# Ordering every engine's work by the scheduler's timeline model in a two-layer RWKV-7 / Conformer backbone

## The chip, the cores and the metric

The kernel runs on one core of a Trainium2 chip. The metric is the device time of one execution in microseconds (us); less is better. A core has a matrix engine (PE), a vector engine (DVE), an activation engine (ACT), GpSimd (POOL) and SyncE (SP), each with an instruction stream of its own that it works off strictly in order. The engines meet only at semaphores. SP and POOL mostly issue DMAs. So for a program whose instructions are given, the order of the instructions on each engine is what is left to choose.

## What is computed

The model has two layers over 512 latent tokens and a prefix of 256 context tokens, D = 1024, all in fp32 at the interface. Layer 0 is the even mixer; it has sixteen heads of 64, which the kernel takes as eight pairs, and a recurrence with a 64x64 state per head, in both directions:

```python
def wkv_scan(S0, r, decay, k, v, kk, a, reverse):
    def step(S, inp):
        r_t, w_t, k_t, v_t, kk_t, a_t = inp
        sa = jnp.einsum("bhvk,bhk->bhv", S, -kk_t)
        S = (S * w_t[:, :, None, :]
             + sa[..., None] * (kk_t * a_t)[:, :, None, :]
             + v_t[..., None] * k_t[:, :, None, :])
        return S, jnp.einsum("bhvk,bhk->bhv", S, r_t)
...
    r, k, v, za, bg, cg, xb, zb = jnp.split(h @ w_in, EVEN_SPLITS, axis=-1)
    ya, _, _ = rwkv_seq(rwkv_prep(h, r, k, v, *rw), S_f, S_b, r_k, lnx_w, lnx_b, True)
    yb = bg * dwconv(cg * xb, sc_w, seg_len)
    y = jnp.concatenate([ya.astype(h.dtype) * jax.nn.silu(za), yb * jax.nn.silu(zb)], axis=-1) @ w_out
```

The context tokens are run first and give the start states S_f and S_b. Layer 1 is a Conformer module (two gated projections, a 31-tap depthwise convolution, a layer norm, an output projection) on the latent tokens alone.

## The kernel before

**Projections.** Each of the eight column groups of h @ w_in (r, k, v, za, bg, cg, xb, zb) is cut into eight blocks of 128 columns. One block is 24 matmuls of 128x512 on PE (`proj`, L361): eight k-tiles, and three products for each, because operands are split into a high and a low fp32r part (`hilo`, L117: a DMA at L123, a cast on ACT at L126, a subtraction on DVE at L127). In the trace the accumulators are called pcg, pxb, pbg and pzb, the operands hlh, hll, whxb, wlxb and so on.

**The recurrence.** It is worked in chunks of 64 tokens. Four context stages of four steps come first (two head pairs each, `chain_ctx`, L689), then eight latent stages of eight steps (one head pair each, `chain_lat`, L739). One latent step is a chain through three engines, and the next step needs its end:

```python
cmm(zo..., AR[z]..., H...)   # then cmm(zo..., E..., UV...)
S.copy(Zs, zo[:, 0:2, :])    # ACT, L758, Ol<-zol in the trace
cmm(uh..., E..., Zs...)
S.copy(UV..., uh...)         # ACT, L764
cmm(uh..., BKt..., UV...)
V.scalar_tensor_tensor(out=Hn..., in0=uh..., scalar=PC..., in1=HP...)   # DVE, L771
```

All matmuls of these chains are pinned to one written order over all stages (`cmm`); so are the masks' products pa (L589 to L601) and the transposes pb (L605 to L612) of each stage.

**What runs beside a chain.** While stage s walks its eight steps, the program has a triangular solve for stage s+1 (`solve`, L642: a transpose at L650, which needs four copies Nt that ACT makes at L618 from all eight E tiles of DVE's L601, then 31 pairs of a product at L656 and a sum at L658 on DVE, each needing the one before), the merge of the solved blocks (L662 to L683), the operands of stage s+2 (`light`, `heavy`, L434 to L636: decay scan L521, products L531 to L556, masks L601, transposes), the finish of stage s (group norm, L795 to L815), and the four projections of one block of the convolution branch (`conv_branch`, L825: cg, xb, bg, zb; L837 takes pxb, L841 twice does the taps, L847 takes pbg, L792 makes the gate from pzb, L850 ends it).

**What sets the order.** The kernel is written against a tile framework. It records the instructions with their data dependences; a list scheduler then picks, for each engine, the next ready instruction by a model of how long each takes, and the program's place among the instructions breaks ties. What holds in any order: the data dependences, the buffers' reuse, the pinned chains, and the few `tc.issue_after` anchors, which forbid an instruction to be placed before an instruction of the chain (CONV_AFTER = (0, 2, 7, 6): cg not before step 0, xb not before step 2, bg not before step 7, zb not before step 6; LIGHT_AFTER and HEAVY_AFTER do the same for the operands of stage s+2). The anchors set a lower bound and no upper one.

**The end.** The output projection of layer 0 has two passes over 16 k-tiles with 12 matmuls each (L130); the first pass needs no result of the last stage but for its last k-tile and lies beside it. Layer 1 follows (L975 to L1245).

## Time and profile before

| | |
|---|---|
| median of three runs | 1452.06 us (1447.48 to 1453.27) |
| the profiled execution | 1451.59 us, of which span 1449.6 us |
| mean granted PE clock | 0.979 |
| setup, first projections (0 to 224.6 us) | 224.6 us |
| four context stages (224.6 to 525.2 us) | 300.6 us |
| seven latent stages (525.2 to 928.3 us) | 403.1 us |
| last latent stage (928.3 to 957.3 us) | 29.0 us |
| rest of the output projection (957.3 to 1040.2 us) | 82.9 us |
| layer 1 (1040.2 us on) | 409.4 us |

The limits are the starts of the first matmul of each stage's chain, read from the trace; that of the output projection's end is the first matmul of layer 1. In a row of the trace, `L771` is the line, `Hl<-uh,PCl,HPl` the tile written and those read (numbers left out), then the shape, the count, the busy time and the mean in ns, and behind the last bar the idle time of the engine just before these instructions with what ended it. A PE row's duration is longer than the time that it takes from PE, since matmuls are pipelined; the distance between two starts is that time.

### The profile page before, as it was taken

Reading aid. Unit: us, or ns where it says so; the run is one execution under the profiler, and the core shown is the slowest. Engines: PE = TensorE matmul, PEld = TensorE weight load, DVE = VectorE, ACT = ScalarE, POOL = GpSimd, SP = SyncE. Lnnn points to the kernel's source line nnn. Section 1 sums busy time; section 2 is a strip of 40 time slices with the busy share of each in tenths; the row PEclk is TensorE's granted clock in tenths of the full one; section 3 lists DMA queues with packets and bytes.
Section 4 is the critical chain, followed back from the end, with each engine's and each line's share of the span. In section 5 each row is a group of like instructions: output and inputs, shape, how many; then the busy total and the mean of one; then the engine's idle time right before and its main releaser. Section 6 shows DMA issues by size and latency. Waiting matters only on the chain. (4 is left out here: it accounts for less than half of the span.)

```text
span 1449.6 us, 29729 instructions
## 1 busy us (share of the span) xinstructions
PE 1407.2 (97%) x11921; PEld 1012.7 (70%) x11921; DVE 983.7 (68%) x2294; ACT 749.5 (52%) x1516; POOL 118.2 (8%) x246
## 2 busy tenths in 40 slices
PE   6999999999998999999999999999999999999998
PEld 1564677878776766666676666778777777788876
DVE  2675597568688989999999998557745544544333
ACT  4536364364664665756666565456753323464222
POOL 2023210000101101011011100010000000000000
PEclk9999999979897999999999999999999999999999
DMA  9755433312222321222222212359803303133322
GB/s 324 221 172 160 153 110 98 97 52 71 83 85 74 92 69 59 81 86 60 76 67 83 91 49 84 131 175 324 252 34 102 117 22 95 58 102 91 99 89 86
DMA packets 137626, 158.54 MB, mean 109 GB/s; under 512 B 15375, under 2 KB 104143, under 8 KB 137369
## 3 DMA queue, kind: packets, MB, share of 16 engines
q1 hardware_dynamic: 121104, 106.47, 23.6%
q0 software_dynamic: 15312, 48.99, 10.5%
q8 instruction: 94, 1.54, 0.4%
q10 hardware_dynamic: 1072, 1.19, 0.2%
q14 instruction: 44, 0.36, 0.1%
HBM read 138.33 MB, written 18.28 MB: 108 GB/s over the span
## 5 line engine op out<-in xcount | busy, mean ns | idle before, releaser
L57 PE MATMUL o<-wh,y 128*128 128x512 f32 x248 | 79.7, 397 | 0.0
L658 DVE TENSOR_TENSOR Yl<-Yl,xtmpl 128x126 f32<-128x126 f32 (+22 forms) x248 | 62.2, 251 | 2.7
L656 DVE TENSOR_TENSOR xtmpl<-Xl,Yl 128x126 f32<-128x126 f32 (+22 forms) x248 | 62.0, 250 | 2.7
L57 PE MATMUL pal<-ARl,BKl 64*128 64x128 f32 x512 | 57.8, 306 | 5.5 <-DVE xtmpc L656 2.8
L57 PEld LDWEIGHTS pal<-ARl,BKl 64*128 64x128 f32 x512 | 42.9, 195 | 24.9 <-issue 6.0
L1140 ACT CAST ah<-a 64x512 fp32r<-64x512 f32 x32 | 19.8, 619 | 75.6 <-DVE a L1135 75.2
L57 PE MATMUL zol<-UV,E 64*64 64x64 f32 (+1 forms) x1024 | 54.0, 221 | 0.2 <-ACT UV L764 0.2
L57 PEld LDWEIGHTS o<-wh,y 128*128 128x128 f32 x248 | 45.9, 188 | 9.5
L764 ACT COPY UV<-uh 64x128 f32<-64x128 f32 x128 | 33.3, 260 | 33.5 <-PE uh L57 25.9
L57 PE MATMUL o<-wl,y 128*128 128x512 f32 x124 | 49.4, 398 | 1.2 <-DVE wl L127 1.2
L57 PE MATMUL zol<-Hl,ARl 64*64 64x64 f32 x896 | 50.2, 230 | 0.3
L57 PEld LDWEIGHTS zol<-Hl,ARl 64*64 64x64 f32 x896 | 35.0, 133 | 20.3 <-issue 16.7
L127 DVE TENSOR_TENSOR wl<-wr,wh 128x1024 fp32r<-128x1024 f32 x28 | 34.2, 1223 | 19.6 <-ACT wh L126 19.1
L1135 DVE TENSOR_TENSOR a<-pu,a 128x512 f32<-128x512 f32 x16 | 11.0, 690 | 53.0 <-PE pu L57 50.7
L57 PEld LDWEIGHTS uh<-UV,BKt 128*64 128x64 f32 x704 | 26.7, 138 | 28.5 <-ACT UV L764 23.1
L601 DVE TENSOR_TENSOR E<-pal,maskE 128x512 f32<-128x512 f32 x64 | 43.0, 685 | 3.4 <-PE pal L57 3.0
L57 PEld LDWEIGHTS zol<-UV,E 64*64 64x64 f32 (+1 forms) x1024 | 42.3, 136 | 2.5 <-ACT UV L764 2.0
L1095 DVE SCALAR_TENSOR_TENSOR pr<-px,dbe,What 119x512 f32<-119x512 f32 x32 | 22.6, 745 | 31.1 <-PE px L57 31.1
L126 ACT CAST wh<-wr 128x1024 fp32r<-128x1024 f32 x28 | 29.6, 1056 | 20.7 <-PE o L57 10.4
L771 DVE SCALAR_TENSOR_TENSOR Hl<-uh,PCl,HPl 128x64 f32<-128x64 f32 x112 | 26.4, 277 | 20.1 <-PE uh L57 9.6
L875 POOL DMA_DIRECT2D mwr<-in_mod_w_dram x56 | 29.9, 538 | 114.2 <-PE uh L57 67.4
L57 PE MATMUL uh<-UV,BKt 128*64 128x64 f32 x704 | 36.7, 234 | 2.2 <-ACT UV L764 2.2
(947 smaller groups left out, 4250.9 us busy)
## 6 DMA issues: line engine op xcount, KB each, us to landing
mwr<-in_mod_w_dram POOLq DMA_DIRECT2D x56, 256.0 KB, 3.6
wr<-in_ev_w_out_dram SPq DMA_DIRECT2D x28, 512.0 KB, 5.6
ectx<-in_mod_w_dram SPq DMA_DIRECT2D x12, 512.0 KB, 5.2
wrk<-in_ev_w_in_dram SPq DMA_DIRECT2D x16, 256.0 KB, 3.1
wrv<-in_ev_w_in_dram SPq DMA_DIRECT2D x16, 256.0 KB, 4.6
wrr<-in_ev_w_in_dram SPq DMA_DIRECT2D x16, 256.0 KB, 2.9
wrza<-in_ev_w_in_dram SPq DMA_DIRECT2D x16, 256.0 KB, 2.8
wrcg<-in_ev_w_in_dram SPq DMA_DIRECT2D x16, 256.0 KB, 2.8
```

The costliest lines, as they stand in the source:

```text
L57: return T.matmul(o, lhsT, rhs, start=start, stop=stop)
L126: S.copy(hi, raw)
L127: env["lo"].tensor_tensor(out=lo, in0=raw, in1=hi, op=ALU.subtract)
L601: V.tensor_tensor(out=E[:, h, z * NLAT + c0 : z * NLAT + c0 + m, :], in0=pas[h], in1=maskE[:, z * (1 + h) : z * (1 + h) + 1, 0:x].to_broad ...
L656: V.tensor_tensor(out=tv, in0=X[:, :i, i : i + 1].to_broadcast([P, i, m]), in1=Y[:, i : i + 1, c0:].to_broadcast([P, i, m]), op=ALU.mult)
L658: V.tensor_tensor(out=Y[:, :i, c0:], in0=Y[:, :i, c0:], in1=tv, op=ALU.add)
L764: u_ = S.copy(UV[ZR[1 - h], i : 2 * nch - i : 2 * nch - 1 - 2 * i, ZR[h]], uh[ZR[1 - h], 0:2, :])
L771: h_ = V.scalar_tensor_tensor(out=Hn[:, z, :], in0=uh[:, 2 + z, :], scalar=PC[z][:, i : i + 1], in1=HP[:, z, :], op0=ALU.mult, op1=ALU.add)
L875: nc.gpsimd.dma_start(mws[q], I["mod_w"][layer, kt * P : (kt + 1) * P, c0 : c0 + 512])
L1095: V.scalar_tensor_tensor(out=pr[s][:NPROD], in0=px[s][:NPROD], scalar=dbe[:, 0:1], in1=What[:, n * 512 : n * 512 + 512], op0=ALU.add, op1= ...
L1135: V.tensor_tensor(out=a, in0=pp[1], in1=a, op=ALU.mult)
L1140: S.copy(ahl[s][hr], a[hr])
```

## The change

One argument, in the function that builds the program:

```diff
@@ -1319,7 +1319,7 @@
     out = nc.dram_tensor("out_0_dram", (1, SEQ, D), F32, kind="ExternalOutput").ap()
-    with _tile.TileContext(nc) as tc:
+    with _tile.TileContext(nc, schedule_with_timeline_sim=True) as tc:
         tile_backbone_kernel(tc, aps, out)
```

The list scheduler stays; the model behind it is another one, with a timeline of its own for each engine. Every instruction of the kernel is there as before: PE's 8217 matmuls, DVE's and ACT's instructions, the DMAs. The pinned chains and the anchors hold as before. What differs is the order of each engine's stream, and with it some semaphore instructions. On PE the runs of fp32r matmuls (the projections) between fp32 ones (the chains and the stages' operands) are 394 before and 210 now.

The first place is PE in latent stage 3, step 2. zol3_2 is the chain's first product in this step, uh0<-Ol3 its second, uh0<-UV110 with BKt its third; pcg4 and pxb4 are projections of the convolution branch. Before:

```order
L57 MATMUL zol3_2_7905<-UV110_5057,E110_5058 64x64 x4
L57 MATMUL pcg4_8511<-hll_119,whcg40_8500 128x512
L57 MATMUL pcg4_8511<-hlh_118,wlcg40_8501 128x512
L57 MATMUL pcg4_8511<-hlh_118,whcg40_8500 128x512
L57 MATMUL pcg4_8511<-hll_119,whcg40_8500 128x512
L57 MATMUL uh0_123<-Ol3_7834,E110_5058 64x64 x4
L57 MATMUL zol3_2_7905<-Hl3_1_7894,ARl30_6576 64x64 x2
L57 MATMUL zol3_2_7905<-Hl3_1_7894,ARl31_6606 64x64 x2
L57 MATMUL pcg4_8511<-hlh_118,wlcg40_8501 128x512
L57 MATMUL pcg4_8511<-hlh_118,whcg41_8506 128x512
L57 MATMUL uh0_123<-UV110_5057,BKt111_5060 64x64 x2
```

The same place now, with twenty of the 24 rows of pxb4 left out at the mark:

```order
L57 MATMUL zol3_2_7905<-UV110_5057,E110_5058 64x64 x4
L57 MATMUL pxb4_8550<-hlh_118,whxb40_8539 128x512
L57 MATMUL pxb4_8550<-hll_119,whxb40_8539 128x512
...
L57 MATMUL pxb4_8550<-hll_119,whxb41_8545 128x512
L57 MATMUL pxb4_8550<-hlh_118,wlxb41_8546 128x512
L57 MATMUL uh0_123<-Ol3_7834,E110_5058 64x64 x4
L57 MATMUL zol3_2_7905<-Hl3_1_7894,ARl30_6576 64x64 x2
L57 MATMUL zol3_2_7905<-Hl3_1_7894,ARl31_6606 64x64 x2
L57 MATMUL uh0_123<-UV110_5057,BKt111_5060 64x64 x2
L57 MATMUL uh0_123<-UV110_5057,BKt110_5059 64x64 x2
L57 MATMUL zol3_2_7905<-UV110_5057,E110_5058 64x64 x4
```

Before, the projections stand in pieces of two to four between the chain's products of every step; now the block of 24 stands whole inside one step, and steps 3 and 4 have none. Over the eight steps of this stage PE has 24, 4, 24, 0, 4, 0, 24 and 24 fp32r matmuls, where it had 5, 6, 9, 9, 9, 2, 6 and 58.

The second place is DVE behind the last update of the state in the same stage, Hl3_6. Yl4, xtmpl4 and Xl4 belong to the solve for stage 4, ARl51 and BKl51 are operands of stage 5. Before:

```order
L771 SCALAR_TENSOR_TENSOR Hl3_6_8069<-uh0_123,PCl31_6598,HPl3_6_8037 128x64
L784 TENSOR_TENSOR Ol3_7834<-zol3_6_8045,Ol3_7834 128x2x64
L656 TENSOR_TENSOR xtmpl4_8107<-Xl4_8105,Yl4_8106 128x78
L554 TENSOR_TENSOR ARl51_8264<-rl5_8177,Pl51_8251 128x8x64
L658 TENSOR_TENSOR Yl4_8106<-Yl4_8106,xtmpl4_8107 128x6x13
L555 SCALAR_TENSOR_TENSOR BKl51_8265<-al51_8249,iPl51_8253 128x8x64
L656 TENSOR_TENSOR xtmpl4_8107<-Xl4_8105,Yl4_8106 128x70
L556 TENSOR_TENSOR BKl51_8265<-kdl51_8258,iPl51_8253 128x8x64
L784 TENSOR_TENSOR Ol3_7834<-zol3_7_8077,Ol3_7834 128x2x64
L658 TENSOR_TENSOR Yl4_8106<-Yl4_8106,xtmpl4_8107 128x5x14
```

The same place now; pzb4 and pbg4 are the projections that PE has in the steps 6 and 7:

```order
L771 SCALAR_TENSOR_TENSOR Hl3_6_8069<-uh0_123,PCl31_6598,HPl3_6_8037 128x64
L784 TENSOR_TENSOR Ol3_7834<-zol3_6_8045,Ol3_7834 128x2x64
L683 COPY E100_4354<-uh1_124 32x16x32
L127 TENSOR_TENSOR wlcg50_9330<-wrcg50_9328,whcg50_9329 128x512
L792 SCALAR_TENSOR_TENSOR gzb4_8655<-gzb4_8655,pzb4_8630 128x512
L127 TENSOR_TENSOR wlcg51_9336<-wrcg51_9334,whcg51_9335 128x512
L847 TENSOR_TENSOR yb4_8576<-pbg4_8592,yb4_8576 128x512
L601 TENSOR_TENSOR E110_5058<-pal5010_8348,maskE_108 128x512
L601 TENSOR_TENSOR E110_5058<-pal5011_8349,maskE_108 128x512
L784 TENSOR_TENSOR Ol3_7834<-zol3_7_8077,Ol3_7834 128x2x64
```

The solve of stage 4 is over before Hl3_4 now, and its merge ends with L683 right behind Hl3_6. The masks L601 of stage 5, which were the second and fourth row behind Ol3<-zol3_7, stand behind L792 and L847; L847 stood 42 rows behind Ol3<-zol3_7 before. Behind the transpose L650 of stage 5 the pairs of its solve stand one after the other now, with only two rows of other work among the 22 rows up to Hl4_0.

## The prediction, made before the changed kernel had run

> **What bounds the kernel now.** I read the page's busy times first, then a table of windows by stage, then the timeline inside one latent stage.
>
> ```profile
> PE 1407.2 (97%) x11921; PEld 1012.7 (70%) x11921; DVE 983.7 (68%) x2294; ACT 749.5 (52%) x1516; POOL 118.2 (8%) x246
> ```
>
> By this row PE bounds the kernel. The windows (columns: window, its length, then busy time and instruction count of PE, weight loads, DVE, ACT and POOL, the granted clock, the DMA share, GB/s) say otherwise for the middle:
>
> ```profile
> core 0: us, PE busy (x) PEld busy (x) DVE busy (x) ACT busy (x) POOL busy (x), PEclk, DMA share, GB/s
> 224.60:525.20 300.60, 290.37 (x2817) 225.91 (x2816) 231.68 (x591) 156.94 (x326) 25.87 (x47) 0.91 0.26 79
> 525.20:587.60 62.40, 58.92 (x760) 40.77 (x759) 54.76 (x157) 42.61 (x100) 6.72 (x12) 1.00 0.22 66
> 706.60:765.00 58.40, 57.48 (x773) 40.11 (x772) 53.49 (x155) 37.60 (x90) 6.70 (x12) 1.00 0.26 77
> 928.30:957.30 29.00, 28.71 (x393) 18.89 (x392) 14.91 (x32) 18.56 (x51) 1.08 (x2) 1.00 0.67 223
> 957.30:1040.20 82.90, 80.98 (x418) 65.30 (x418) 59.17 (x91) 55.85 (x102) 4.83 (x9) 1.00 0.77 267
> 1040.20:1449.60 409.40, 403.44 (x1809) 309.74 (x1807) 183.34 (x240) 155.30 (x233) 3.17 (x6) 1.00 0.28 86
> ```
>
> The fourth row is latent stage 3: 58.4 us, DVE busy for 53.5. PE is busy for 57.5 there, but that is the sum of records of pipelined matmuls. What a block takes from PE shows in layer 1, in the chain that ended last:
>
> ```profile
> 1066.79 5.79 PE pu L57 x24
> ```
>
> 24 matmuls of 128x512 take 5.8 us, 0.24 each; the timeline inside a stage has records of 0.40 for such a matmul, 0.23 apart:
>
> ```profile
> 651.46 0.50 PE L57 MATMUL pcg<-hlh,whcg 128*128 128x512 f32 x1
> ...
> 652.03 0.39 PE L57 MATMUL pcg<-hlh,wlcg 128*128 128x512 f32 x1
> 652.26 0.40 PE L57 MATMUL pcg<-hlh,whcg 128*128 128x512 f32 x1
> ```
>
> So PE's 97% is mostly overlap, and in the latent stages DVE and the chain set the time. DVE's own pace and the chain's hops are the two prices needed:
>
> ```profile
> 652.22 0.43 DVE L771 SCALAR_TENSOR_TENSOR Hl<-uh,PCl,HPl 128x64 f32<-128x64 f32 x2
> ...
> 652.82 0.45 PE L57 MATMUL zol<-Hl,ARl 64*64 64x64 f32 x8
> ...
> 653.56 0.27 ACT L758 COPY Ol<-zol 128x128 f32<-128x128 f32 x1 [0.28 <-PE zol L57]
> ...
> 654.10 0.27 PE L57 MATMUL uh<-Ol,E 64*64 64x64 f32 x2
> ...
> 654.59 0.53 ACT L764 COPY UV<-uh 64x128 f32<-64x128 f32 x2 [0.77 <-PE uh L57]
> ...
> 655.18 0.45 PE L57 MATMUL uh<-UV,BKt 128*64 128x64 f32 x8
> ...
> 655.76 0.47 DVE L771 SCALAR_TENSOR_TENSOR Hl<-uh,PCl,HPl 128x64 f32<-128x64 f32 x2
> ```
>
> ```profile
> 699.55 0.68 DVE L127 TENSOR_TENSOR wlzb<-wrzb,whzb 128x512 fp32r<-128x512 f32 x1
> 700.15 0.16 DVE L428 SCALAR_TENSOR_TENSOR orq<-orq 128x8 f32<-128x8 f32 x1
> ...
> 701.54 0.21 DVE L658 TENSOR_TENSOR Yl<-Yl,xtmpl 128x31 f32<-128x31 f32 x1
> 701.78 0.20 DVE L656 TENSOR_TENSOR xtmpl<-Xl,Yl 128x30 f32<-128x30 f32 x1
> 702.02 0.21 DVE L658 TENSOR_TENSOR Yl<-Yl,xtmpl 128x30 f32<-128x30 f32 x1
> ```
>
> From update to update of the state H a nearly unfilled step takes 3.5 us (652.22 to 655.76); whatever PE puts between these rows comes on top. On DVE a record of 0.68 is followed after 0.60 if the next instruction doesn't read its result (0.08 less than the record), and one of 0.21 after 0.24 if it does (0.03 more).
>
> **The change part by part.** Nothing is added or removed; every term comes from order. I take the update H of each step as the milestone and walk through the seven intervals of latent stage 3 in the new order. In each, the later of two things ends: what DVE has queued ahead of the next update, or the chain with what PE has inside it. Durations of kinds not yet shown:
>
> ```profile
> L601 DVE TENSOR_TENSOR E<-pal,maskE 128x512 f32<-128x512 f32 x64 | 43.0, 685 | 3.4 <-PE pal L57 3.0
> ...
> L521 DVE TENSOR_TENSOR_SCAN Pl<-scm,sg 128x528 f32<-128x528 f32 x16 | 20.1, 1253 | 1.8 <-ACT sg L513 1.5
> L650 DVE STREAM_TRANSPOSE Xl<-Nt 128x1024 f32<-128x1024 f32 x8 | 16.3, 2038 | 1.5 <-ACT Nt L618 1.4
> ...
> L664 DVE STREAM_TRANSPOSE kdml<-Yl 128x512 f32<-128x512 f32 x8 | 9.0, 1122 | 0.0
> ```
>
> ```profile
> L618 ACT COPY Nt<-E 32x512 f32<-32x512 f32 x32 | 19.7, 617 | 16.7 <-DVE E L601 16.3
> ```
>
> ```profile
> L658 DVE TENSOR_TENSOR Yl<-Yl,xtmpl 128x126 f32<-128x126 f32 (+22 forms) x248 | 62.2, 251 | 2.7
> ```
>
> - H0 to H1, DVE: the two updates 0.5, 15 solve instructions of about 0.28, two of 128x512 at 0.7, four small ones at 0.17, 6.8 in records; at its pace 5.9 us.
> - H1 to H2, DVE: eleven of 128x512, a scan of 1.25, eleven solve instructions, seven small ones and the updates, 13.5 in records, 31 neighbours mostly independent at 0.08 less: 10.9.
> - H2 to H3, DVE: twelve solve instructions of about 0.21, two taps of 0.75, the updates: 4.3. The 24 pxb matmuls stand inside this chain's step 2, but their 5.8 us pass while DVE is in the 10.9 before, so they cost nothing unless DVE is quicker there than I count.
> - H3 to H4: DVE has one solve pair, 0.7; the chain needs 3.5, with no projection to fill it. DVE waits about 3.
> - H4 to H5, DVE: O, the scan, eight of 128x512, the merge's transposes and copies (1.1, 0.7, 0.8) and the updates, 9.0 at its pace and 0.8 of waiting for ACT ahead of the scan: 9.8.
> - H5 to H6, chain: 3.5 and twelve pzb matmuls inside it at 0.23, 2.7: 6.2. DVE has 1.8 and waits for the rest.
> - H6 to the next stage's H0, DVE: 22 of about 128x512, L650, eleven small ones, 20 solve instructions, O twice and the updates, 25 in records, 23.4 at its pace. To that come waits that this order puts ahead of everything else. L792 needs pzb, whose second half PE has only behind step 6's chain (2.2 us). L847 needs pbg, which starts behind zol3_7: 24 matmuls, 5.8, with the chain's products between them, against some 1.2 of DVE work left (4.7). The masks L601 and all that hangs on them are queued behind it. L650 needs four Nt copies of 0.62 behind the last mask, and only one other instruction could cover them: none stands there (2.5). Together 32.8.
>
> The sum is 73.4 us where the trace has 58.4: 15.0 more. DVE's work is only some 3.5 of it, because the solve, whose pairs depend on each other, was interleaved with other work and now runs in rows; the rest are waits that the old order covered. Bounds per stage: 5, if only the pace counts and half of one gap stays, and 20, if a second wait behind L847 opens. Stages 1 to 5 have the same order: 5 × 15 = **+75** (25 to 100). Stage 0, counted in the same way, comes to 74 against 62.4: **+12** (5 to 20). Stage 6 has nothing to prepare: **+1**.
>
> The context stages gain. The switch between projection and chain on PE costs about 0.1 (the first pcg matmul above has a record of 0.50, later ones 0.40), and some 110 of the switches saved lie before 525.2: 11 us. Their clock of 0.91 over 300.6 us loses 27 us, seen in the windows on PE:
>
> ```profile
> 300.00:310.00 10.00, 7.08 (x119) 0.90 0.10 31
> 310.00:320.00 10.00, 10.00 (x129) 0.50 0.26 80
> 440.00:450.00 10.00, 6.36 (x41) 0.90 0.36 106
> 450.00:460.00 10.00, 10.00 (x166) 0.50 0.34 107
> ```
>
> After ten microseconds in which PE idled for 3 to 4, the clock is 0.50 for the next ten. The new context steps have 25 to 140 projection matmuls each where the short ones had 13 to 22, so I give back a third of the 27, 9 us: together **−20** (−45, if all of it and the waits go, to +15, if the masks there come as late as in the latent stages).
>
> The same rows price the new idle time. Between H4 and H5 PE has 3.5 us of chain and some 1.5 of pa in 9.8: an idle stretch of 4 to 6 us, once in each stage, ahead of a chain-bound interval. Half clock there doubles the 2.7 of pzb: **+10** over stages 1 to 5 as far as it isn't hidden (0 to 25). The Trainium skill ("TensorE: Matmul & The Clock Gate", Part 1: The HAM clock gate) says that the clock falls to half after an idle window of about 3.4 us and returns after a busy one of that length. The rows above agree with the fall; by the return in 3.4 us this term would be near its lower end.
>
> The last latent stage and the projection behind it: the first pass of the output projection stands whole before the second step now, and steps 2 to 7 have nothing between their products. Two rows of the page give PE's work:
>
> ```profile
> L57 PE MATMUL o<-wh,y 128*128 128x512 f32 x248 | 79.7, 397 | 0.0
> ...
> L57 PE MATMUL o<-wl,y 128*128 128x512 f32 x124 | 49.4, 398 | 1.2 <-DVE wl L127 1.2
> ```
>
> 372 matmuls at 0.24 are 89 us, seven steps at 3.5 are 24.5: 114 in a row against the 111.9 of the two windows (29.0 and 82.9). I take **0** (−15, as part of the first pass is done in stage 6, to +25, if the weights' DMAs come late: the second of these windows has a DMA share of 0.77). Layer 1 keeps its order but for details: 0.
>
> The queues of SP and POOL are reordered too: small loads of the recurrence's second-layer weights stand earlier among the loads of the modulation weights, and stores of the context states later, behind weight loads.
>
> ```profile
> wrcg<-in_ev_w_in_dram SPq DMA_DIRECT2D x16, 256.0 KB, 2.8
> ```
>
> A weight block lands in 2.8 us, and the latent window has a DMA share of 0.26, so the loads, a projection block (5.8) ahead, hide: 0, and at worst 2.8 for each of the few blocks that come behind such a store.
>
> Sum against the profiled execution's 1451.6, which is within 0.5 of the median: 1451.6 + 75 + 12 + 1 − 20 + 10 + 0 = **1530 us**.
>
> **The rivals.** *PE is the bound after all, faster.* Then the 368 saved switches at 0.1 count in full, 37 us, and the walk above is wrong because DVE's waits are filled: 1415. For it speaks the page's 97%; against it DVE's 53.5 of 58.4. The Trainium skill ("Perfetto Trace Analysis", Matmul Optimizations) asks for matmuls back to back in batches, which is what this order does; in layer 1, where PE really bounds, the trace agrees. Chance 0.15.
>
> *No change.* The latent stages lose only the pace, 3.5 each (21 over six), and the context stages give 20 back: 1452. It needs the waits at L847 and L792 to vanish, as they would if pbg were done before Hl3_6; the order forbids that for pbg. Chance 0.08.
>
> *Much slower.* The idle stretch lowers the clock for the whole second half of each stage, and the chain's hops and the pbg block, 5.8, double: 10 more per stage, over 1590. In the trace low clock lasted 7 to 20 us after such a stretch; the latent stages had none. Chance 0.07.
>
> **How the numbers follow.** The forecast, 1465 to 1590, has 0.70. About 0.5%, 7 us, is what a measurement of this kernel can tell from no change. Faster by more: 0.16 (the first rival and a little of the second); within: 0.07; slower: 0.77. The range reaches from 1440, which leaves out most of the first rival, to 1585: sums of all low ends (1417) and all high ends would need every term to miss on one side.
>
> **What the profile would show.** Right: latent stages of 70 to 77 us with DVE's busy time still near 54; DVE idle ahead of L847 and L792 for PE (pbg, pzb), ahead of L650 for ACT, ahead of L771 in the steps 4 and 6 for PE's uh; a granted clock below 1.00 in some latent windows; context stages of about 280. Wrong: latent stages near 58 or below with DVE's waits filled; or a loss that lies in the context stages or in the tail.

## The result, and the profile after

The changed kernel takes 1640.03 us (median of four runs, 1638.79 to 1640.93), before takes 1451.3 in the same comparison: the ratio is 1.1306, with a 95% interval of 1.1291 to 1.1321. The forecast was 1530, with a range up to 1585. The direction was right, the size was not.

The busy times of the page after:

```profile
PE 1455.8 (89%) x11921; PEld 1089.2 (66%) x11921; DVE 999.1 (61%) x2294; ACT 752.3 (46%) x1516; POOL 118.1 (7%) x246
```

The same instructions, DVE busy for 15 us more than before, and PE's records cover 89% of the span instead of 97%: most of the 189 us more of the span is waiting, and part of it is half clock on PE, as shown below. Where they lie shows in the windows of after, cut at the first matmul of each chain (columns as before; the seventh latent stage, the sixth from zero, is the fifth row of numbers):

```profile
core 0: us, PE busy (x) PEld busy (x) DVE busy (x) ACT busy (x) POOL busy (x), PEclk, DMA share, GB/s
0.00:186.10 186.10, 163.44 (x796) 86.71 (x796) 89.80 (x170) 85.77 (x154) 38.77 (x102) 0.98 0.63 202
186.10:521.00 334.90, 311.87 (x3070) 245.84 (x3068) 264.25 (x702) 180.03 (x375) 31.14 (x57) 0.94 0.29 86
521.00:607.00 86.00, 68.66 (x872) 52.69 (x873) 61.09 (x163) 40.03 (x94) 6.69 (x12) 0.83 0.19 55
772.50:854.50 82.00, 65.62 (x774) 50.58 (x774) 57.29 (x156) 37.87 (x89) 6.71 (x12) 0.79 0.17 53
1016.20:1093.00 76.80, 68.42 (x778) 52.40 (x780) 49.93 (x132) 36.30 (x83) 2.15 (x4) 0.90 0.32 105
1093.00:1224.30 131.30, 110.94 (x793) 88.00 (x789) 64.21 (x109) 64.45 (x137) 5.88 (x11) 0.87 0.53 181
1224.30:1638.60 414.30, 397.84 (x1769) 304.79 (x1767) 183.26 (x240) 157.18 (x233) 3.17 (x6) 0.98 0.26 83
```

| | before | after | difference | forecast |
|---|---|---|---|---|
| to the first latent stage | 525.2 | 521.0 | -4.2 | -20 |
| latent stage 0 | 62.4 | 86.0 | +23.6 | +12 |
| latent stages 1 to 5 | 295.6 | 409.2 | +113.6 | +75, and +10 for the clock |
| latent stage 6 | 45.1 | 76.8 | +31.7 | +1 |
| last chain to the last matmul of the output projection | 111.6 | 131.3 | +19.7 | 0 |
| layer 1 | 409.7 | 414.3 | +4.6 | 0 |

(The layers are parted here at the last matmul of the output projection, 1039.9 before and 1224.3 after, since in the new order the first matmuls of layer 1 start ahead of it.)

Latent stage 3 again: 82.0 us instead of 58.4, DVE busy for 57.3 instead of 53.5, so DVE idles for 24.7 us in place of 4.9. Its waits in that stage, after (waiting instruction, what it waited for; total, times, longest):

```profile
DVE wlzb L127 <- ACT whzb L126: 5.0, 1, 5.0
DVE Hl L771 <- ACT sg L511: 4.8, 1, 4.8
DVE wlcg L127 <- ACT whcg L126: 4.0, 2, 2.1
DVE yb L847 <- PE pbg L57: 2.2, 1, 2.2
DVE Xl L650 <- ACT Nt L618: 2.0, 1, 2.0
```

The wait of L771 is put down to an activation, sg; that was long done, and the real one is the chain through PE. The first and third are new: in before this stage has no wait at L127 among those listed, and none longer than 0.8 us. The timeline of DVE and ACT behind step 5 shows what they are; DVE first:

```profile
831.90 0.69 DVE L127 TENSOR_TENSOR wlzb<-wrzb,whzb 128x512 fp32r<-128x512 f32 x1 [4.95 <-ACT whzb L126]
833.41 0.47 DVE L771 SCALAR_TENSOR_TENSOR Hl<-uh,PCl,HPl 128x64 f32<-128x64 f32 x2 [0.81 <-PE uh L57]
...
837.35 0.69 DVE L127 TENSOR_TENSOR wlcg<-wrcg,whcg 128x512 fp32r<-128x512 f32 x1 [1.85 <-ACT whcg L126]
838.08 0.69 DVE L792 SCALAR_TENSOR_TENSOR gzb<-gzb,pzb 128x512 f32<-128x512 f32 x1
840.88 0.69 DVE L127 TENSOR_TENSOR wlcg<-wrcg,whcg 128x512 fp32r<-128x512 f32 x1 [2.11 <-ACT whcg L126]
843.78 0.69 DVE L847 TENSOR_TENSOR yb<-pbg,yb 128x512 f32<-128x512 f32 x1 [2.21 <-PE pbg L57]
844.39 1.28 DVE L601 TENSOR_TENSOR E<-pal,maskE 128x512 f32<-128x512 f32 x2
```

```profile
831.25 0.62 ACT L126 CAST whzb<-wrzb 128x512 fp32r<-128x512 f32 x1 [4.34 <-PE pzb L57]
...
840.22 0.62 ACT L126 CAST whcg<-wrcg 128x512 fp32r<-128x512 f32 x1 [2.24 <-PE pbg L57]
```

DVE stands at the subtraction of a weight block (L127), which needs ACT's cast (L126), which waits until PE's projection is through with an older block in the same buffer. Everything queued behind it on DVE, the masks of the stage after next among it, waits too. In the old order these subtractions stood behind the masks.

PE's granted clock over the same stage, in windows cut at its changes:

```profile
772.50:803.10 30.60, 27.25 (x280) 0.89 0.16 46
803.10:813.30 10.20, 6.64 (x84) 0.51 0.10 28
813.30:820.40 7.10, 3.03 (x68) 0.98 0.11 38
820.40:830.50 10.10, 7.99 (x105) 0.50 0.31 106
830.50:848.00 17.50, 15.27 (x192) 0.99 0.17 49
848.00:854.50 6.50, 5.44 (x50) 0.50 0.22 74
```

Ahead of each of the three stretches at half clock PE idles in pieces, the longest of 2.4 us, that come to some 2 to 4 us within 4 to 7; the half clock then lasts 10 to 14 us (the third runs on into the next stage). The stages 1, 2 and 4, with a clock of 0.75 as a whole, have one long stretch of 27 us and one of 14 instead (in stage 4 from 885.3 to 912.6, PE busy for 20.6 us of it, and from 929.6 to 943.3). The forecast had one stretch in a stage, ahead of 2.7 us of projection.

### The profile page after: what moved, and what is told of

It reads as the page before. It is cut to its first block, busy times and chain, and to the rows that moved or that the text cites. A ratio compares the mean times of both kernels' runs of the same rounds, so it can differ in the third digit from the quotient of the medians.

```text
span 1638.6 us, 29755 instructions
## 1 busy us (share of the span) xinstructions
PE 1455.8 (89%) x11921; PEld 1089.2 (66%) x11921; DVE 999.1 (61%) x2294; ACT 752.3 (46%) x1516; POOL 118.1 (7%) x246
## 5 line engine op out<-in xcount | busy, mean ns | idle before, releaser
L57 PE MATMUL zol<-Hl,ARl 64*64 64x64 f32 x896 | 62.2, 271 | 28.5 <-DVE Hl L771 25.6
L57 PE MATMUL pal<-ARl,BKl 64*128 64x128 f32 x512 | 67.4, 377 | 19.0 <-DVE E L601 18.1
L57 PEld LDWEIGHTS pal<-ARl,BKl 64*128 64x128 f32 x512 | 54.7, 263 | 27.5 <-DVE E L601 21.4
L57 PEld LDWEIGHTS zol<-Hl,ARl 64*64 64x64 f32 x896 | 45.2, 168 | 38.8 <-issue 15.8
L57 PE MATMUL uh<-UV,BKt 128*64 128x64 f32 x704 | 42.2, 258 | 28.4 <-ACT UV L764 27.5
L57 PE MATMUL zol<-UV,E 64*64 64x64 f32 (+1 forms) x1024 | 66.6, 261 | 0.7 <-ACT UV L764 0.7
L771 DVE SCALAR_TENSOR_TENSOR Hl<-uh,PCl,HPl 128x64 f32<-128x64 f32 x112 | 26.5, 278 | 59.0 <-PE uh L57 30.8
L57 PEld LDWEIGHTS uh<-UV,BKt 128*64 128x64 f32 x704 | 31.1, 159 | 42.9 <-ACT UV L764 33.5
L57 PEld LDWEIGHTS zol<-UV,E 64*64 64x64 f32 (+1 forms) x1024 | 54.9, 174 | 3.0 <-ACT UV L764 2.8
L601 DVE TENSOR_TENSOR E<-pal,maskE 128x512 f32<-128x512 f32 x64 | 41.2, 683 | 9.1 <-PE pal L57 6.8
L618 ACT COPY Nt<-E 32x512 f32<-32x512 f32 x32 | 19.7, 616 | 57.4 <-DVE E L601 57.2
L127 DVE TENSOR_TENSOR wl<-wr,wh 128x1024 fp32r<-128x1024 f32 x28 | 34.2, 1223 | 18.1 <-ACT wh L126 18.1
L1095 DVE SCALAR_TENSOR_TENSOR pr<-px,dbe,What 119x512 f32<-119x512 f32 x32 | 22.6, 746 | 34.9 <-PE px L57 34.8
L57 PEld LDWEIGHTS uh<-Ol,E 64*64 64x64 f32 x512 | 24.3, 161 | 27.8 <-issue 13.4
```

The costliest lines, as they stand in the source:

```text
L57: return T.matmul(o, lhsT, rhs, start=start, stop=stop)
L127: env["lo"].tensor_tensor(out=lo, in0=raw, in1=hi, op=ALU.subtract)
L601: V.tensor_tensor(out=E[:, h, z * NLAT + c0 : z * NLAT + c0 + m, :], in0=pas[h], in1=maskE[:, z * (1 + h) : z * (1 + h) + 1, 0:x].to_broad ...
L618: S.copy(Nt[rs], E[rs, h, :, 32 * b : 32 * b + 32])
L771: h_ = V.scalar_tensor_tensor(out=Hn[:, z, :], in0=uh[:, 2 + z, :], scalar=PC[z][:, i : i + 1], in1=HP[:, z, :], op0=ALU.mult, op1=ALU.add)
L1095: V.scalar_tensor_tensor(out=pr[s][:NPROD], in0=px[s][:NPROD], scalar=dbe[:, 0:1], in1=What[:, n * 512 : n * 512 + 512], op0=ALU.add, op1= ...
```

## The experiments

In most of them an engine's rows are held to a given order. A table holds the numbers of its instructions, and an edge without a semaphore ties each to the one ahead of it; the scheduler orders the engines that are not held. The first runs have all five engines held to the order after, with one thing altered. The helper is shortened here.

```diff
-    with _tile.TileContext(nc, schedule_with_timeline_sim=True) as tc:
+    with _tile.TileContext(nc) as tc:
         tile_backbone_kernel(tc, aps, out)
+        _in_order(tc, ORDER_PE)     # and DVE, ACT, POOL, SP
...
+def _in_order(tc, text):
+    here = {i.name: i for i in tc.nc.cur_bb.bb.instructions}
+    row = [f"I-{n}" for n in _names(text)]
+    for a, b in zip(row, row[1:]):
+        tc.add_manual_dep(here[b], a, NoSync, reason="order")
```

The two orders can't be mixed freely: PE's rows of one with DVE's rows of the other, both held, wait for each other in a circle. So when one engine is held below, the others do not keep the rows that they have in before or after. A run with before's order in which only PE's blocks are gathered to 24 is not among them.

**The clock.** The order after, with matmuls that keep PE busy:

```diff
-                chain_lat(st, i)
+                chain_lat(st, i) or i < NLAT - 1 or s > 9 or _warm(mm, uhs, ident, s - 4, "ab")
...
-                merge(sts[s + 1])
+                merge(sts[s + 1]) or not 4 <= s < 10 or _warm(mm, uhs, ident, s - 4, "c")
...
+WARM = dict(a1=5, a2=10, b0=4, b1=9, b2=7, c1=4, c2=6)
+def _warm(mm, uhs, ident, p, which):
+    for place, n in WARM.items():
+        if place[0] in which:
+            DUM[f"{place}{p}"] = [mm(uhs[1][:, 0:128], ident, ident, True, True).ins.name for _ in range(n)]
```

> The order after, row for row on every engine, with 45 extra 128x128 matmuls of the identity into an unused PSUM bank in each of the latent stages 0 to 5, put where PE stood idle (steps 2, 5 and behind step 7); they compute nothing that is used. Theory A, the clock: PE idles for 3 to 6 us three times a stage and then runs at half clock for some 30 of 82 us, which stretches the chain-bound intervals; with PE kept busy the granted clock in these stages goes from 0.75-0.79 to over 0.9 and a stage from 82 to about 74 us, the sum of the walk through the seven intervals: 6 x 8 = 48 us, to about 1592. Theory B, waits alone: the low clock is a symptom of the waits and costs nothing that the waits do not cover; the clock rises and the time stays at 1640 +-5.

Measured: 1625.63 us (two runs, 1620.67 and 1630.59), 14 less. The clock came back fully only in stage 5; in stages 1 to 4 it is 0.93 to 0.95. The windows of stages 4 and 5 of this run:

```profile
848.40:924.10 75.70, 67.93 (x864) 53.85 (x865) 57.31 (x157) 38.00 (x89) 6.74 (x12) 0.95 0.20 58
924.10:999.10 75.00, 65.47 (x867) 51.85 (x867) 57.06 (x157) 37.07 (x88) 3.36 (x6) 1.00 0.16 50
```

They take 75.7 and 75.0, where after has 81.5 and 80.2. So the half clock is worth some 5.5 us a stage there, 3 to 4 in stages 1 to 3, stage 0 even lost 2.5, and with a clock of 1.00 a stage still has 16 us more than before. Theory A is right about what the clock does and had too much for the sum; the waits are the larger part.

**The block in step 7.** The order after, with pbg's 24 matmuls moved on PE:

```diff
-CONV_AFTER = (0, 2, 7, 6)
+CONV_AFTER = (0, 2, 3, 6)
```

> The order after, except that in the latent stages 0 to 5 the 24 pbg matmuls are moved on PE from step 7 into the steps 3, 4 and 5, eight each (the anchor of pbg is moved from step 7 to step 3); DVE, ACT, POOL and SP keep their rows. Theory A, the place of the block: step 7's chain and all masks behind L847 lose the 5.8 us block, and the steps 3 to 5 fill their idle time with it: 8 to 12 us a stage, about 1570 to 1590. Theory B, DVE's own order (the solve in rows, L650 behind the last mask) sets the stage: 2 us a stage at most, about 1628.

Measured: 1626.26, 14 less, the number of theory B. The stretch from the last update to the next stage's first fell, but the update of step 3 came 2 to 3 us later, since eight matmuls stood in its chain. Both repairs together, with 50 extra matmuls:

> The run with pbg in the steps 3 to 5, with 50 extra matmuls of the identity in each of the stages 0 to 5 where PE still stood idle; they compute nothing that is used. Theory A, block and clock add up: each alone gave some 14 us, and here the low clock that was left (0.88 in a stage) goes too, so that a stage takes about 72 us: about 1598. Theory B, the two repair the same waits: no more than 5 us below the better of the two, about 1621. In neither does a stage come back to 58.4, since DVE's slower pace (3.8 a stage) and the waits for the weights' casts stay.

Measured: 1615.61, between the two theories and nearer to B. Over the whole kernel the two repairs nearly add up, 24 us together and 14 and 14 apart. But stages 1 to 5 take 75.0 to 77.1, and in stages 4 and 5, where the extra matmuls alone had already come to 75.7 and 75.0, the moved block wins nothing further (75.0 and 77.1). There the two repair the same waits.

**Stage 6 and the output projection.** Two splices: the order after up to a point, before's from there. The cut goes through before's own order of issue, so that nothing waits in a circle. First at latent stage 6, then at stage 7; in words:

```diff
+S = rows that before had issued ahead of the first matmul of zol6_0     # zol7_0
+rows of S in the order after, then the others in before's order
```

> The order after for everything that before had issued ahead of latent stage 6, and before's order from there on. Theory A, the loss from stage 6 to the end of the output projection (about 51 us in the two traces) is made there, by blocks of 24 inside a chain that nothing else hides and by the output projection's weights not loading during the last chain: all of it comes back, about 1589. Theory B, it is handed on from stage 5 (late operands): half comes back, about 1615.

Measured: 1601.63, 38 less, between the two theories. Stage 6 takes 49.3 (45.1 in before), the last chain with the output projection 111.3 up to layer 1's first matmul (111.8 in before), but stage 5 takes 90.9 instead of 80.2: it has 15 more DVE instructions and 72 more matmul records in it than in after, work that the new order had still left to do.

> The order after for everything that before had issued ahead of latent stage 7 (stage 6 keeps its blocks of 24), and before's order from there on, which puts the first pass of the output projection beside the last chain again. Theory A, both parts lose: the stage 6 keeps some 20 of its 31 us, the rest of the 51 comes back: about 1610. Theory B, only the output projection's place matters: all comes back, about 1589. Theory C, only stage 6 matters: about 1635.

Measured: 1610.40, 30 less: theory A. Stage 6 with its blocks takes 68.1. The reverse splice tells whether the loss was handed on:

> Before's order for everything that after had issued ahead of latent stage 6, and the order after from there on: the other half of the splice at stage 6. Theory A, the loss behind stage 6 belongs to that part alone: 1451 and the 51 us that lie there between the two traces, about 1502. Theory B, only the 38 us that the first splice gave back belong to it, the rest is handed on from stage 5: about 1489.

Measured: 1505.86, 55 more than before: theory A. The order from stage 6 on loses it by itself: 34 us in stage 6, 19 up to the end of the output projection, 4 in layer 1. How the last chain loses shows in its windows in the trace of after (PE busy, clock, DMA share, GB/s):

```profile
1118.00:1124.00 6.00, 6.00 (x41) 1.00 0.48 162
1124.00:1130.00 6.00, 3.54 (x84) 0.80 0.01 3
1130.00:1136.00 6.00, 4.42 (x74) 0.50 0.00 0
1136.00:1142.00 6.00, 4.25 (x76) 0.50 0.01 3
1142.00:1148.00 6.00, 3.93 (x56) 0.50 0.00 0
1148.00:1154.00 6.00, 1.65 (x31) 0.50 0.01 3
1154.00:1160.00 6.00, 3.93 (x16) 0.50 0.38 116
1160.00:1166.00 6.00, 6.00 (x24) 0.85 0.95 273
```

With the first pass of the output projection done ahead of step 2, the buffers for its weights are not freed while the chain walks alone: for 30 us next to nothing is loaded, at half clock, and then the second pass waits for DMAs that run at 270 to 400 GB/s. That is read from the windows; no run has this part alone.

**Which engine's rows.** PE's rows of after under before's model:

```diff
     with _tile.TileContext(nc) as tc:
         tile_backbone_kernel(tc, aps, out)
+        _in_order(tc, ORDER_PE)     # the rows of after
```

> The model of before, with the order of PE alone held to the rows of after; DVE, ACT, POOL and SP are ordered by the model of before around it. Theory A, PE's blocks of 24 carry the loss, and any model must queue the other engines around them: 1620 to 1650. Theory B, the loss is in what the timeline model does to DVE: the old model finds better places for the solve and the masks, below 1560.

Measured: 1652.34, 2 above the range of theory A. PE's rows alone are enough for a loss of 201 us; but the counterpart overturned what I had read into it. PE's rows of before under the timeline model:

> The counterpart of the run with PE's rows alone: the timeline model of after orders DVE, ACT, POOL and SP, and PE is held to before's rows. Theory A, the loss sits in PE's rows and the other engines follow them: within 10 us of before, 1441 to 1461. Theory B, the timeline model costs time on DVE whatever PE does: 1500 or more.

Measured: 1598.22, the ratio 1.0996 (1.0944 to 1.1047). Theory B: with PE's order unchanged, the timeline model's rows on the other engines cost 148 us. These rows are not those of after, and the loss lies elsewhere: 45 us of it ahead of the first latent stage (570.3 against 525.2), where after itself loses nothing, 69 in stages 1 to 5 (after: 114), 6 in stage 6 (after: 32). And DVE's rows of after with PE left to before's model:

> The model of before with DVE alone held to the rows of after; PE is free, but comes out with 272 runs of fp32r matmuls (394 before, 210 after), most blocks whole. Theory A, either engine's rows drag the other's along, because DVE's rows hold the weights' casts and the readers of the blocks: 1600 to 1650. Theory B, with PE free the old model fills the chain's steps and only DVE's part of the loss shows: 1520 to 1570.

Measured: 1784.96, beyond both. Either engine's rows are enough to lose by. The third test of the blocks cuts them up within the timeline model:

```diff
-    def proj(wt, o, h):
+    def proj(wt, o, h, at=(None,) * 8):
         for kt in range(KT):
...
-            mm3(o, wh[:, ks], wl[:, ks], h[0][:, kt, :], h[1][:, kt, :], kt == 0, kt == KT - 1)
+            with after(at[kt]):
+                mm3(o, wh[:, ks], wl[:, ks], h[0][:, kt, :], h[1][:, kt, :], kt == 0, kt == KT - 1)
...
-            proj(wt, pcg, hlat)
+            proj(wt, pcg, hlat, at(0, 2))
```

> The timeline model as in after, with the convolution branch's anchors set for each k-tile instead of each block, so that a block cannot stand in one step: in a latent stage PE's steps have 6 to 18 fp32r matmuls each (after: 24, 4, 24, 0, 4, 0, 24, 24); DVE's rows stay close to those of after. Theory A, whole blocks in a step (and the empty steps and the low clock that go with them) make the loss: stages of 62 to 66 us and a clock near 1.00, 1500 to 1540. Theory B, DVE's order makes it (the solve early and in rows, the masks queued behind the projections' readers), and PE's pieces only change where PE waits: a few us a stage, about 1610.

Measured: 1619.62, nearer to theory B: 20 us come back, and the stages still take 75 to 82. So the loss doesn't need whole blocks inside the chain. How the 189 us divide between PE's rows and those of the others these runs don't tell: either is enough alone, and when one is held, the others move.

One difference on DVE with PE held to before's rows (1598 us) is the place of the solve. In the stages 1 to 6 of before its 62 rows stand in 46 to 57 pieces, mostly single rows with other work between, over 128 to 139 rows of DVE's stream. In the order after they stand in 23 to 25 pieces of up to 20 rows, over 99 to 108; with PE's rows of before held, in 24 to 41 pieces over 99 to 134. The rows pushed back for it are the updates H, the sums O and the masks. Two runs with PE held to before part DVE from ACT, and a third the DMAs from ACT:

```diff
     with _tile.TileContext(nc, schedule_with_timeline_sim=True) as tc:
         tile_backbone_kernel(tc, aps, out)
+        _in_order(tc, ORDER_PE)     # before's rows
+        _in_order(tc, ORDER_ACT)    # DVE in the second run, DVE and ACT in the third
```

> PE and ACT held to before's rows; the timeline model orders DVE, SP and POOL. In the run with PE alone held, DVE's rows differ from before's in one way above all: the solve's pairs stand 12 rows earlier in the mean (up to 51), and the updates H, the masks and the O sums up to 38 rows later. Theory A, that is the loss: within 15 us of that run, 1583 to 1613. Theory B, it is ACT's rows (casts of weights ahead of the chain's copies): below 1500.

Measured: 1542.14, 93 more than before, between the two theories. In the profiled execution, 85 us longer than the profiled one of before, 35 of them lie ahead of the first latent stage and 34 in stages 1 to 5.

> PE and DVE held to before's rows; the timeline model orders ACT, SP and POOL. Theory A, DVE's rows are the loss: 1450 to 1465. Theory B, ACT's rows or the order of the DMAs: above 1540.

Measured: 1495.66, 46 more: neither range held it. 93 and 46 come to 139 of the 148, but the order of the DMAs, which both runs leave to the timeline model, is counted twice in that.

> PE, DVE and ACT held to before's rows; the timeline model orders only SP and POOL, that is the DMAs. The run with ACT, SP and POOL free cost 46 us. Theory A, those 46 us are ACT's rows (the weights' casts and the solve's and merge's copies out of place): 1449 to 1460. Theory B, they are the order of the DMAs (loads of weights behind stores): 1480 to 1496.

Measured: 1455.71, the ratio 1.0039 (1.0005 to 1.0072): theory A, so by subtraction some 40 of the 46 are ACT's rows. Which of ACT's rows was not taken further.

**The solve in bursts, alone.** Before's order on every engine; on DVE the solve's rows are gathered, twelve at the place of the first of them, or all 62:

```diff
 L656 TENSOR_TENSOR xtmpl4<-Xl4,Yl4
+L658 TENSOR_TENSOR Yl4<-Yl4,xtmpl4
+L656 TENSOR_TENSOR xtmpl4<-Xl4,Yl4
...
 L554 TENSOR_TENSOR ARl51<-rl5,Pl51
-L658 TENSOR_TENSOR Yl4<-Yl4,xtmpl4
```

> Before's order on every engine, except that on DVE the solve of each latent stage (62 rows, each needing the one before) is gathered into bursts of twelve rows, each at the place of its first; nothing else is moved. Theory A, a burst of some 3 us stands ahead of the updates H and the masks, and the chain waits for it on top of DVE's slower pace: 1490 to 1530. Theory B, only the pace of dependent neighbours counts, 0.12 us for each of some 35 to 40 in a stage: 1475 to 1485.

Measured: 1536.14, 87 more than before, above the range of theory A. Stage 3 of this run takes 68.9 with nothing else moved:

```profile
758.20:827.10 68.90, 63.19 (x773) 44.02 (x772) 56.83 (x150) 37.75 (x89) 6.15 (x11) 0.90 0.19 55
```

DVE is busy for 3.3 us more (56.8 against 53.5), which is the pace of dependent neighbours; the other 7.2 of the 10.5 are waits, and a clock of 0.90 where before had 1.00. Theory B would have only the 3.3.

> The same with the whole solve of a stage in one burst behind its transpose L650. Theory A: H of step 0 waits for 15 us of solve, and the steps behind it cannot win this back, since each takes 3.5 us of chain at the least: 10 to 15 us a stage, 1530 to 1570. Theory B, only the pace: 1475 to 1490.

Measured: 1595.36, 146 more than before, again above the range. In some stages a whole solve now runs one stage earlier than in before, as two neighbouring windows of this run show:

```profile
857.30:953.60 96.30, 61.95 (x773) 42.21 (x772) 73.30 (x203) 37.59 (x90) 7.26 (x13) 0.81 0.17 51
953.60:1012.30 58.70, 58.28 (x773) 39.93 (x772) 46.71 (x110) 36.76 (x88) 3.22 (x6) 1.00 0.24 72
```

The stage with two solves takes 96.3. The next has 7.8 us less DVE work than in before and still takes 58.7: what a stage loses, its neighbour doesn't win back.

**A version faster than both.** Before's order, with 42 extra matmuls of the identity in five places of the context stages, built like the first experiment:

```diff
-                merge(sts[s + 1])
+                (s < 3 and _warm(mm, uhs, ident, s)) or merge(sts[s + 1])
+WARM = ((("g1", 8), ("g2", 8)), (("g3", 8),), (("g4", 14), ("g5", 4)))
```

> Before's order, row for row, with 42 extra 128x128 matmuls of the identity on PE in five places of the context stages where it idles just ahead of a half-clock stretch (they compute nothing that is used). Theory A, the half clock of these stretches (51 us of them) delays what bounds the stages there: the clock of 0.89 to 0.90 in context stages 1 to 3 goes to 1.00 and 10 to 20 us are won, 1431 to 1441. Theory B, DVE sets those stages and the half clock is hidden: 1451 +-3. Theory C, the extra matmuls themselves lie in the way: up to 1460.

Measured: 1440.49 (twelve runs against seventeen of before), the ratio to before 0.9931 (0.9907 to 0.9956): theory A, at the small end of its gain. The windows of the context stages 1 to 3, before and then with the extra matmuls:

```profile
290.20:366.60 76.40, 72.97 (x731) 59.17 (x730) 55.38 (x145) 38.35 (x83) 3.26 (x6) 0.89 0.20 62
366.60:427.60 61.00, 59.10 (x633) 44.63 (x632) 46.79 (x117) 36.25 (x79) 7.31 (x13) 0.89 0.30 87
427.60:525.20 97.60, 92.70 (x915) 68.82 (x914) 86.00 (x215) 56.45 (x108) 11.51 (x21) 0.90 0.27 81
```

```profile
290.80:360.70 69.90, 69.06 (x763) 55.94 (x762) 55.20 (x145) 38.56 (x83) 3.25 (x6) 1.00 0.22 67
360.70:416.80 56.10, 55.19 (x651) 41.55 (x650) 46.13 (x116) 35.05 (x78) 7.28 (x13) 1.00 0.32 94
416.80:510.50 93.70, 90.75 (x951) 68.27 (x950) 86.23 (x215) 57.32 (x110) 11.48 (x21) 0.98 0.29 84
```

The clock goes from 0.89 to 0.90 up to 0.98 to 1.00, and 6.5, 4.9 and 3.9 us are won, by work that nobody reads.

## Why the prediction was right in direction and wrong in size

**The bound.** Right in what it ruled out: putting PE's matmuls together didn't make the kernel faster, and the rival in which PE bounds (1415) fell. That DVE's work sets a stage was too simple, though: with 46.7 us of it a stage of before's order takes 58.7 all the same (the second window of the last burst run), and there PE's records cover 58.3. So chain and projections need as long as DVE; which of them sets the time no run tells.

**The walk through the seven intervals.** Right but for the clock. Between the first updates of the steps, from the starts of L771 in stage 3 of the traces, and in stage 5 of the run with extra matmuls, whose clock is 1.00:

| interval | before | forecast | after | extra matmuls |
|---|---|---|---|---|
| H0 to H1 | 4.1 | 5.9 | 6.6 | 6.6 |
| H1 to H2 | 4.1 | 10.9 | 11.1 | 10.5 |
| H2 to H3 | 4.3 | 4.3 | 4.4 | 4.3 |
| H3 to H4 | 4.3 | 3.5 | 5.6 | 4.0 |
| H4 to H5 | 4.7 | 9.8 | 9.9 | 10.1 |
| H5 to H6 | 3.6 | 6.2 | 8.9 | 6.3 |
| H6 to the next H0 | 33.5 | 32.8 | 34.9 | 33.6 |
| sum | 58.6 | 73.4 | 81.4 | 75.4 |

The two intervals that the chain sets, H3 to H4 and H5 to H6, are the two that miss by more than 2, besides the last; with the clock held at 1.00 they come out at 4.0 and 6.3. The column of before, which the walk didn't set beside its own, shows where the loss sits: all but 1.4 us of it lies in the six steps, and the last interval is as long as it was. The two that grew by DVE's queue are H1 to H2 and H4 to H5. DVE hardly idles in them; the windows of after, then of before, with the last interval as third row (columns as before):

```profile
793.50:804.60 11.10, 7.56 (x78) 5.86 (x72) 11.09 (x33) 7.92 (x18) 0.00 (x0) 0.94 0.08 24
814.60:824.50 9.90, 4.33 (x100) 3.69 (x98) 9.30 (x17) 6.19 (x14) 2.45 (x5) 0.79 0.17 57
833.41:868.34 34.93, 31.45 (x280) 24.50 (x276) 23.35 (x58) 12.56 (x27) 1.70 (x3) 0.80 0.18 56
```

```profile
714.65:718.74 4.09, 4.09 (x60) 2.70 (x56) 4.09 (x13) 3.69 (x10) 0.00 (x0) 1.00 0.00 0
727.41:732.12 4.71, 4.53 (x73) 3.43 (x69) 4.19 (x11) 4.56 (x12) 0.46 (x1) 1.00 0.36 105
735.67:769.17 33.50, 32.83 (x430) 23.51 (x427) 31.36 (x82) 18.46 (x36) 5.51 (x10) 1.00 0.29 85
```

What stands ahead of the update there are above all the operands of the stage after next, the scan L521 and the products L531 to L556 in one piece; rows of the solve are eleven of the 33 in the first, under 3 us, and none in the second. The new order took 8 us of DVE's work out of the last interval and put it ahead of these updates, and in the last interval waits took the place of the work. Of those waits the total of 9.4 was right, the names were half wrong: behind L683 it is not L792 but the subtractions of the weights (L127, 4.0 us) that wait.

**The clock term, +10 over stages 1 to 5, was mis-sized.** The step took one idle stretch a stage and doubled 2.7 us of pzb. In that interval it is right (8.9 against the walk's 6.2). But the half clock lies over 34 to 42 us of a stage (its mean clock is 0.75 to 0.79), and where the extra matmuls lift it, in stages 4 and 5, 5.5 us a stage come back, an estimated 27 over the five stages. The stages take 81.8 us in the mean, 8.4 above the walk; the 2.9 that the clock doesn't explain are the walk's own. The return of the clock after about 3.4 us of sustained busy time, which the Trainium skill states ("TensorE: Matmul & The Clock Gate", Part 1: The HAM clock gate) and which would have put the term near its lower end, is not what the trace of before shows: in the row 310 to 320 us of the prediction PE is busy by its records for all ten microseconds (129 matmuls, most of them of 64x64 or 32x32), and the clock stays at 0.50. In after, 803.1 to 813.3 lies at 0.51 with PE busy for 6.6 of 10.2 us, but with pauses.

**Stage 6, +1, failed: +31.7.** This is the largest miss of the sum. The step said that this stage has nothing to prepare. In the new order it has: DVE is busy for 49.9 us in it (33.1 in before), and 12 of the 17 more are the operands of the output projection's first pass (L127). Above all the step left out the blocks of 24 that stand inside its chain: 24, 6, 24, 0, 24, 3, 24 and 55 matmuls in its steps at 0.24 are some 38 us of PE work on top of the chain's 28. The splices show that the order of this stage loses by itself: it keeps 68.1 us when only the part behind it is before's again, and the order from stage 6 on alone costs 55. And it is PE's rows that carry the loss: with those of after under before's model the stage takes 73.0, with those of before under the timeline model 51.1.

**The last chain and the output projection, 0, missed by 19.7, inside its bounds.** The sum of PE work, 114 against 111.9, left out that the weights' loads stop with the buffers. The upper end of 25, given for late DMAs, held it. With PE's rows of before held under the timeline model this part loses 17 us too, so the first pass standing whole ahead of step 2 is not needed for such a loss.

**The context stages, -20, came to -4.2.** The clock is 1.00 in the first three of them; then in the last 63.1 us DVE has 55.6 us of work for the first latent stages, PE idles for 19 of them and the clock falls to 0.68. That is a reading of the trace, no run tested it. **Stage 0, +12, came to +23.6.** The runs with PE's rows of before take 62 to 71 us in it, those with PE's blocks of after 84 to 93; which interval of it the forecast had wrong stays open.

**The cause named, and the cause found.** The prediction laid the loss in a stage to the pace of the solve in rows (3.5 us) and to waits that the old order covered. The pace was about right: 3.8 in stage 3 of after (2.7 in the mean of stages 1 to 5), 3.3 in the burst run. The experiment adds that a burst costs more than its pace, since in an in-order queue it holds up the update that the chain needs: twelve rows at a time, alone, cost 87 us. In after most pieces are shorter and, in the two intervals above, the rows that hold up the update are mostly not the solve's; that these cost in the same way is read from the trace, no run moved them alone. And the losses are not a sum of parts: PE's rows of after alone drag the other engines to 1652, the other engines' rows under the timeline model lose 148 with PE's as before, and cutting PE's blocks up gives 20 back. Why the timeline model orders the rows so was not tested.

**The sum.** The stages 1 to 5 have the greatest loss, 114, of which the forecast had 85. Its sign of being wrong, a loss in the tail, came true for 51 us (stage 6 and behind it) beside that. The measured time is about the sum of the prediction's high ends (1638), which it had held for unlikely. (The low ends as stated come to 1423, not 1417.)

**The third rival,** half clock in the second half of each stage (over 1590, chance 0.07), has a number that the kernel did pass, and about half of each stage does run at half clock. But with the clock lifted the stages 4 and 5 keep 16 of their 21 to 22 us: the number was met for another reason.

## What to carry to other kernels

Read a scheduler's order as queues: find the row that the longest chain needs on each engine, and count what stands ahead of it, in that engine's own measured pace; set it beside what the same stretch takes now, and do it also in the stages where the usual bound has less work, since blocks that hide behind DVE elsewhere lie bare there. On DVE here, rows that each need the one before were better between other work than together. Where PE idles for a few microseconds ahead of a chain, look for half clock behind it (10 to 27 us a stretch in the latent stages here), price it in every interval that the chain sets, and try a handful of matmuls that do nothing.

## What was not expected of the hardware

Extra matmuls made the kernel faster: 42 of them, some 10 us of PE time at 0.23 each, won 0.7% of the whole by keeping the granted clock at 0.98 to 1.00 in stages where it had been 0.89 to 0.90. And half clock outlasts its cause: after idle pieces that come to 2 to 4 us it stayed at 0.50 for 10 to 14 us in stage 3, three times, and for 27 us in the stages 1, 2 and 4, while most of the matmuls that PE was given were small ones, of 64x64 or 32x32.
